# Second gate's seven products: another order, mixes formed inside PSUM banks, partial results subtracted inside the banks, weight rests cast in halves

## The chip, the core and the metric

One core of a Trainium2 chip runs the whole program. The time is the device time in microseconds of one execution; three runs of the kernel before gave 668.48, 669.56 and 670.56, median 669.56. TensorE is written PE, VectorE DVE, ScalarE ACT, GpSimd POOL, SyncE (which issues most DMAs) SP.

## What is computed

The reference is a two-layer encoder over 512 tokens of width 1024: a neighbourhood attention layer, then a latent attention layer. Each layer ends with a gate, and only the gate of the second layer is touched here:

```
h = x + y
gate = jax.nn.sigmoid(rmsnorm(h, ple_norm[i]) @ ple_w_gate[i])
x = h + gate * (p[i] @ ple_w_proj[i])
return rmsnorm(x, final_norm)          # after the second layer
```

## The kernel before

All matrix products are float32 products made of three float32r passes (high x high, low x high, high x low): an operand is a high copy (ACT) and a rest (the difference, by DVE or POOL). One 128 x 512 result is a PSUM bank; the pool tags are `mm` (2 banks), `S` (2), `T` (3), `O` (1).

**The second gate** (`gate_seven`, called for layer 1 from `run`) multiplies the 512 x 1024 state by the 1024 x 1024 weight as a 2 x 2 block product with seven products in place of eight. The state's four quarters are A (tokens 0-255, columns 0-511), B (same tokens, columns 512-1023), C and D (tokens 256-511). The seven left sides are 1: A, 2: B, 7: A-C, 6: A-C+D, 5: C-D, 3: B-(A-C+D), 4: D; the right sides are three quarters of the weight and four sums that DMAs formed in DRAM during the first layer. Each product runs for two row blocks `i` of 128 tokens; each needs 12 matmuls of 512 columns (or 24 of 256).

`keep_half(t, n, ps)` gets each quarter when PE has transposed it into a `T` bank: `out_proj` finishes row block t, column half n, DVE adds the residual (L428), scales it (`hg`, L1022), PE transposes it (L139). `operand(p, i, x)` makes the left side `X[p]`: ACT copies x (L538), DVE subtracts the copy (L539). Before the change the mixes live in one SBUF tile `mix`, named `F`; A-C and A-C+D are formed there (L556, L560), C-D too (L561), and D is copied to SBUF (L562). `mixed(p)` makes the left sides 6, 5, 4, 3 out of SBUF, so there DVE reads two SBUF tiles.

`gate_seven` takes the products in the order 1, 7, 6, 5, 4, 3, 2. `prep(p)` loads two weight pieces per product (SP, L588; three landing buffers `wraw`), ACT copies them (L589), POOL forms the rests (L590, 1024 columns at once): fourteen casts in all. Products 1 and 2 share a bank, so do 6, 5 and 3; what must be subtracted between them is held in SBUF: `s1`, `s17` (DVE, L650), `s6` (ACT L653, POOL L656). `finish` applies the sigmoid (ACT L595), multiplies with `pe` (DVE L598), adds to the residual `res` (DVE L600) and calls `done` at once: sum of squares (ACT L1066), small DVE and POOL steps (L1067, L1076), the scale by the final norm (DVE L1077, ACT L1078) and the output DMA.

Engines run their queues in order; each queue's order is fixed when the program is built, by a scheduler that follows the code, with `issue_after` holding PE's order of products.

Of the kernel before, what the change touches and what calls it, by code (L numbers as in the profile page):

```python
# [13 lines left out]
F32 = mybir.dt.float32  # L14
# [5 lines left out]
P = 128  # L20
# [20 lines left out]
class Trunk:  # L41
# [374 lines left out]
    def out_proj(self, wap, oT, res, after, last_mm):  # L416
        nc = self.nc
        for n in range(2):
            ws = [self.load_w(wap[n, c], 1024, extra=n == 1 or c == 3) for c in range(4)]
            for u, t in enumerate((0, 2, 1, 3) if n and self.wxn > 5 else range(NT)):  # L420
                ps = self.psum(("mm", "mm", "S", "S", "T", "O", "mm", "mm")[n * NT + u])
                L = lambda s, k: oT[s][k // 4][:, k % 4, t * P:(t + 1) * P]
                W = lambda s, k: ws[k // 2][s][:, (k % 2) * S:(k % 2 + 1) * S]
                m = self.by_chunk(L, W)
                with self.tc.issue_after(last_mm):
                    self.last_out = self.mms(ps, m)
                r = res[t][:, n * S:(n + 1) * S]
                nc.vector.tensor_tensor(out=r, in0=ps, in1=r, op=ALU.add)  # L428
                after(t, n)
# [111 lines left out]
    def keep_half(self, t, n, ps):  # L541

        nc = self.nc
        if (t, n) == (0, 0):
            self.X, self.B, self.Dd = {}, {}, {}
            self.F = self.bigtile("mix").bitcast(F32)
        i = t % 2
        ac, c = self.F[:, i, :], self.F[:, 2 + i, :]
        if t < 2:
            self.operand(1 + n, i, ps)  # L550
            if n:
                self.B[i] = self.temp("b")
            nc.scalar.activation(self.B[i] if n else ac, ps, AF.Copy)
        elif n == 0:
            nc.scalar.activation(c, ps, AF.Copy)
            nc.vector.tensor_tensor(out=ac, in0=ac, in1=ps, op=ALU.subtract)  # L556
            self.operand(7, i, ac)
        else:
            self.Dd[i] = self.temp("d")
            nc.vector.tensor_tensor(out=ac, in0=ac, in1=ps, op=ALU.add)  # L560
            nc.vector.tensor_tensor(out=c, in0=c, in1=ps, op=ALU.subtract)  # L561
            nc.scalar.activation(self.Dd[i], ps, AF.Copy)  # L562

    def mixed(self, p):

        for i in range(2):
            if p == 3:
                self.nc.vector.tensor_tensor(out=self.B[i], in0=self.B[i], in1=self.F[:, i, :], op=ALU.subtract)
            self.operand(p, i, {6: self.F[:, i, :], 5: self.F[:, 2 + i, :], 3: self.B[i], 4: self.Dd[i]}[p])

    def gate_seven(self, pool, layer, rh, res, after):
# [6 lines left out]
        def prep(p):  # L578
            nonlocal pieces
            W[p] = []  # L580
            src = self.quarter[layer][p] if p < 4 else self.sums[layer][p]
            for c in range(2):
                own = pieces % turns < 3
                pieces += 1
                raw = self.wp.tile([P, 1024], F32, name="wraw", tag="wraw", bufs=3)
                q, n = (self.wp, 3) if own else (pool, self.wxn)
                hi, lo = (q.tile([P, 1024], F32R, name=t, tag=t if own else "w4", bufs=n) for t in ("whi", "wlo"))
                nc.sync.dma_start(raw, src[c * P:(c + 1) * P])  # L588
                nc.scalar.activation(hi, raw, AF.Copy)  # L589
                nc.gpsimd.tensor_tensor(out=lo, in0=raw, in1=hi.bitcast(F32),  # L590
                                                                             op=ALU.subtract)
                W[p].append((hi, lo))

        def finish(t, n, x, o=0, wd=S):
            nc.scalar.activation(x, x, AF.Sigmoid, scale=rh[t])  # L595
            pe = pool.tile([P, S], F32, name="pe", tag="pe", bufs=4)[:, :wd]
            nc.sync.dma_start(pe, self.pe[layer][t][:, n * S + o:n * S + o + wd])
            nc.vector.tensor_tensor(out=x, in0=pe, in1=x, op=ALU.mult)  # L598
            r = res[t][:, n * S + o:n * S + o + wd]
            nc.vector.tensor_tensor(out=r, in0=r, in1=x, op=ALU.add)  # L600
            after(t, n, o, wd)

        def quarter(t, n, x, ps, other, op):
            nc.vector.tensor_tensor(out=x, in0=ps, in1=other, op=op)
            finish(t, n, x)

        mm = self.last_out
        order = (1, 7, 6, 5, 4, 3, 2)
        whole, parts = ((0, S),), ((0, 256), (256, 256))
        for p in order[:3]:  # L610
            prep(p)
        self.mixed(6)
        warm = self.small.tile([P, 1], F32, name="warm", tag="warm", bufs=1)
        nc.scalar.activation(warm, rh[3], AF.Sigmoid)
        for k, p in enumerate(order):
            if k == 0:
                prep(order[3])
            if k > 1 and k + 2 < len(order):
                prep(order[k + 2])
            if 0 < k < 4:  # L620
                self.mixed(order[k + 2])
            x = self.X[p]
            for i in range(2):
                cuts = parts if layer == 1 and i == 1 and p < 3 else whole
                if p == 1:
                    A[i] = [self.psum("O" if o else "mm") for o, wd in cuts]
                elif p in (7, 6, 4):
                    ps = self.psum({7: "T", 6: "S", 4: "T"}[p])
                    if p == 6:
                        Bk[i] = ps  # L630
                else:
                    ps = Bk[i]
                for h, (o, wd) in enumerate(cuts):
                    if p < 3:
                        ps = A[i][h]
                    m = [(x[:, 2 * s + i, k * P:(k + 1) * P], W[p][k // 2][r][:, k % 2 * S + o:k % 2 * S + o + wd])
                         for c in range(2) for s, r in ((0, 0), (1, 0), (0, 1)) for k in (2 * c, 2 * c + 1)]
                    for j, (l, r) in enumerate(m):
                        with self.tc.issue_after(mm.ins):
                            mm = nc.tensor.matmul(ps[:, :wd], l, r, start=j == 0 and p in (1, 7, 6, 4),  # L640
                                                  stop=j == 11 and p not in (1, 6, 5), skip_group_check=True)
                    if p == 1:
                        if o == 0:
                            s1[i] = self.temp("s1")
                        nc.scalar.activation(s1[i][:, o:o + wd], ps[:, :wd], AF.Copy)
                    elif p == 2:
                        finish(i, 0, ps[:, :wd], o, wd)
                    elif p == 7:
                        s17[i] = self.temp("s17")
                        nc.vector.tensor_tensor(out=s17[i], in0=ps, in1=s1[i], op=ALU.add)  # L650
                    elif p == 6:
                        s6[i] = self.temp("s6")
                        nc.scalar.activation(s6[i], ps, AF.Copy)  # L653
                    elif p == 5:
                        quarter(2 + i, 1, self.psum("T"), ps, s17[i], ALU.subtract)
                        nc.gpsimd.tensor_tensor(out=s6[i], in0=s17[i], in1=s6[i], op=ALU.subtract)  # L656
                    elif p == 4:
                        quarter(2 + i, 0, ps, ps, s6[i], ALU.add)
                    else:
                        quarter(i, 1, ps, ps, s1[i], ALU.subtract)  # L660
# [276 lines left out]
    def run(self):  # L937
# [64 lines left out]
        for layer in range(2):  # L1002
            with tc.tile_pool(name=f"out{layer}", bufs=4, reuse_waits="tile") as pool:
# [48 lines left out]
                else:  # L1052
                    mean = {}

                    def done(t, n, o, w):
# [22 lines left out]
                        nc.scalar.activation(r[:, f], r[:, f], AF.Copy, scale=rs)  # L1078
# [118 lines left out]
```

## Time and profile before

| | us |
|---|---|
| median of three runs | 669.56 |
| the profiled execution | 669.19 |
| its span, first to last instruction | 667.4 |
| first matmul of the second gate starts | 616.19 |
| last matmul ends | 658.58 |
| PE busy | 655.5 |
| POOL busy | 420.8 |
| ACT busy | 422.0 |
| DVE busy | 382.8 |

The span is the time between the first and the last instruction on the core; 1.8 us of the execution lie outside it. Times in the timelines count from the span's start. The granted TensorE clock is 0.997 over the span.

### The profile page before, as it was taken

To read this page: it belongs to the slowest core of one execution; us is meant where nothing else is said; L and a number is where in the kernel's file an instruction comes from. 1 tells how busy PE (TensorE), PEld (TensorE's weight loads), DVE (VectorE), ACT (ScalarE), POOL (GpSimd) and SP (SyncE) were. 2 spreads that over 40 slices of the span, in tenths; PEclk is the share of its full clock that TensorE was granted. 3 is DMA by queue.
4 is the path that set the end of the run, shared out by engine and by line. 5 is a ranking of instruction groups with operands and counts; after the bars stand their busy time and mean duration, and the time that the engine had idled before them with its cause. 6 is when DMAs were issued, how large, how long until landed. Compare 5 with 4: busy or idle time off the path is not lost.

```text
span 667.4 us, 10026 instructions
## 1 busy us (share of the span) xinstructions
PE 655.5 (98%) x3443; PEld 555.3 (83%) x3443; DVE 382.8 (57%) x817; ACT 422.0 (63%) x838; POOL 420.8 (63%) x340
## 2 busy tenths in 40 slices
PE   9999999999999999999999999999999999999994
PEld 6888888988988888888899888888888888888774
DVE  6290375737645514544525614888988875155977
ACT  7671686848767742543443635897989887446845
POOL 0395466876575765843154626786959786848893
PEclk9999999999999999999999999999999999999998
DMA  8949322966142146534243335120211222664423
GB/s 315 350 146 345 145 93 94 202 160 156 59 140 76 64 153 241 190 104 138 94 108 110 107 88 166 32 76 24 68 29 64 64 96 106 235 245 156 174 74 147
DMA packets 37682, 90.63 MB, mean 136 GB/s; under 512 B 4416, under 2 KB 13376, under 8 KB 37568
## 3 DMA queue, kind: packets, MB, share of 16 engines
q1 hardware_dynamic: 33040, 85.02, 37.1%
q0 software_dynamic: 4160, 4.19, 4.0%
q10 hardware_dynamic: 432, 0.79, 0.3%
q8 instruction: 27, 0.44, 0.3%
q14 instruction: 23, 0.19, 0.1%
HBM read 78.45 MB, written 16.78 MB: 143 GB/s over the span
## 4 chain that ended last, share of the span: by engine, by line
PE 91%; DVE 3%; ACT 2%; DMA 2%; issue 1%; POOL 1%; POOLq 0%; ACTq 0%
PE ps_mm L107 42%; PE ps_S L107 13%; PE ps_mm L727 7%; PE ps_T L139 6%; PE ps_O L838 4%; PE ps_T L107 3%; PE ps_O L107 3%; PE ps_T L238 2%; PE ps_O L402 2%; PE ps_mm L184 2%; PE ps_T L390 2%; PE ps_S L354 1%; PE ps_S L353 1%; PE ps_O L238 1%; DMA wraw<-gate 1%
## 5 line engine op out<-in xcount | busy, mean ns | idle before, releaser
L84 POOL TENSOR_TENSOR wwlo<-wraw,wwhi 128x1024 fp32r<-128x1024 f32 (+5 forms) x93 | 178.2, 1929 | 106.4 <-ACT wwhi L83 90.1
L83 ACT ACTIVATE wwhi<-wraw 128x1024 fp32r<-128x1024 f32 (+5 forms) x94 | 79.1, 863 | 73.6 <-issue 18.2
L823 POOL TENSOR_TENSOR ex<-ex,rc 128x512 f32<-128x512 f32 x64 | 66.3, 1046 | 25.2 <-DVE rc L822 18.1
L821 ACT ACTIVATE ex<-ps_S,mx 128x512 f32<-128x512 f32 x64 | 44.0, 687 | 12.2 <-DVE mx L819 11.1
L819 DVE TENSOR_REDUCE mx<-ps_S 128x1 f32<-128x512 f32 x64 | 43.7, 683 | 7.2 <-PE ps_S L107 6.8
L96 DVE TENSOR_TENSOR pt_lo<-ps_T,pt_hi 128x512 fp32r<-128x512 f32 x64 | 43.3, 682 | 7.7 <-ACT pt_hi L94 7.3
L376 POOL TENSOR_TENSOR ex<-ex,rc 128x128 f32<-128x128 f32 (+1 forms) x64 | 34.8, 583 | 18.1 <-DVE rc L372 18.1
L107 PE MATMUL ps_mm<-xh,wwhi 128*128 128x512 f32 x152 | 40.8, 399 | 0.0
L94 ACT ACTIVATE pt_hi<-ps_T 128x512 fp32r<-128x512 f32 x64 | 37.7, 594 | 4.4 <-PE ps_T L139 4.2
L139 PE MATMUL ps_T<-ident,ex 128*128 128x128 f32 x256 | 38.4, 272 | 0.0
L107 PE MATMUL ps_mm<-xl,wwhi 128*128 128x512 f32 x152 | 38.2, 390 | 0.0
L107 PE MATMUL ps_mm<-xh,wwlo 128*128 128x512 f32 x152 | 38.1, 391 | 0.0
L590 POOL TENSOR_TENSOR wlo<-wraw,whi 128x1024 fp32r<-128x1024 f32 x14 | 36.6, 2636 | 2.3 <-issue 2.3
L139 PEld LDWEIGHTS ps_T<-ident,ex 128*128 128x128 f32 x256 | 31.5, 140 | 7.7 <-POOL ex L823 0.4
L107 PE MATMUL ps_mm<-wwhi,hnT 128*128 128x512 f32 x128 | 35.5, 396 | 0.0
L205 DVE TENSOR_TENSOR u<-ps_O,u 64x512 f32<-64x512 f32 x32 | 21.9, 686 | 20.2 <-ACT u L204 19.7
L107 PEld LDWEIGHTS ps_mm<-xl,wwhi 128*128 128x128 f32 x152 | 28.4, 188 | 5.8
L107 PEld LDWEIGHTS ps_mm<-xh,wwlo 128*128 128x128 f32 x152 | 28.3, 188 | 5.8
L370 ACT ACTIVATE ex<-ex,mx 128x128 f32<-128x128 f32 (+1 forms) x64 | 30.3, 475 | 1.8 <-DVE mx L360 0.8
L107 PEld LDWEIGHTS ps_mm<-xh,wwhi 128*128 128x128 f32 x152 | 27.4, 188 | 4.7
L107 PE MATMUL ps_S<-ke,qe 96*128 96x512 f32 x96 | 29.2, 410 | 0.1
L107 PE MATMUL ps_S<-ko,qo 128*128 128x512 f32 x96 | 28.9, 409 | 0.0
(432 smaller groups left out, 1783.5 us busy)
## 6 DMA issues: line engine op xcount, KB each, us to landing
wraw<-na_qk SPq DMA_DIRECT2D x16, 512.0 KB, 3.3
pe<-pe SPq DMA_DIRECT2D x31, 256.0 KB, 2.8
wraw<-gate SPq DMA_DIRECT2D x14, 512.0 KB, 3.3
wraw<-na_v SPq DMA_DIRECT2D x8, 512.0 KB, 3.3
wraw<-na_o SPq DMA_DIRECT2D x8, 512.0 KB, 3.2
wraw<-mla_z SPq DMA_DIRECT2D x8, 512.0 KB, 3.5
wraw<-mla_o SPq DMA_DIRECT2D x8, 512.0 KB, 3.4
wraw<-sum SPq DMA_DIRECT2D x8, 512.0 KB, 3.2
```

Source lines behind the costliest of these rows:

```text
L83: nc.scalar.activation(hi[:, c], raw[:, c], AF.Copy)
L84: f = lambda e, c=c: e.tensor_tensor(out=lo[:, c], in0=raw[:, c], in1=hi[:, c].bitcast(F32), op=ALU.subtract)
L94: self.last_copy = nc.scalar.activation(hi, src, AF.Copy, scale=scale)
L96: nc.vector.tensor_tensor(out=lo, in0=src, in1=hi.bitcast(F32), op=ALU.subtract)
L107: last = self.last_mm = nc.tensor.matmul(out, l, r, start=i == 0, stop=i == n - 1)
L139: self.last_mm = self.nc.tensor.transpose(t[:, i * P:(i + 1) * P], b, self.ident)
L376: self.last_norm = nc.gpsimd.tensor_tensor(out=e, in0=e, in1=rc[:, qt:qt + 1].to_broadcast([P, e.shape[1]]), op=ALU.mult)
L590: nc.gpsimd.tensor_tensor(out=lo, in0=raw, in1=hi.bitcast(F32), op=ALU.subtract)
L727: self.last_mm = nc.tensor.matmul(PS[key], *terms[i], start=i == 0, stop=i == len(terms) - 1)
L819: nc.vector.reduce_max(mx, sp, axis=AX.X, negate=True)
L821: nc.scalar.activation(ex, sp, AF.Exp, bias=mx, accum_out=sm)
L823: nc.gpsimd.tensor_tensor(out=ex, in0=ex, in1=rc.to_broadcast([P, S]), op=ALU.mult)
```

## The change

Up to 596 us of the profiled execution the instructions of both programs stand in the same order on every engine. Behind that point:

- `out_proj` takes the row blocks 0, 1, 2, 3 in the second column half (before 0, 2, 1, 3).
- The mixes are formed in the `T` bank that PE transposed into: A-C overwrites the bank (L554), D's left side is made straight from its bank, then A-C+D overwrites it (L560) and gives left side 6 straight from the bank. C-D and B-(A-C+D) go to SBUF temporaries `c` and `b`.
- The products come in the order 1, 7, 2, 6, 5, 3, 4. Product 4 accumulates onto product 7's banks, product 3 onto 6+5. Between them DVE changes the banks in place (L616, L641), in place of `s6` on POOL.
- Halves of 256 columns are now used for products 7 and 4 at i = 1 (before: 1 and 2).
- Each weight rest is cast on POOL as two instructions of 512 columns (L589).
- `finish` calls `done` only behind the next sigmoid. The add to `res` goes to POOL (L603), but to DVE for products 3 and 4; the last scale of two row blocks goes from ACT to POOL (L1082).

```diff
-            for u, t in enumerate((0, 2, 1, 3) if n and self.wxn > 5 else range(NT)):
+            for u, t in enumerate(range(NT)):
...
         elif n == 0:
+            c = self.C[i] = self.temp("c")
             nc.scalar.activation(c, ps, AF.Copy)
-            nc.vector.tensor_tensor(out=ac, in0=ac, in1=ps, op=ALU.subtract)
-            self.operand(7, i, ac)
+            nc.vector.tensor_tensor(out=ps, in0=self.AC[i], in1=ps, op=ALU.subtract)
+            self.operand(7, i, ps)
+            nc.scalar.activation(self.AC[i], ps, AF.Copy)
         else:
-            self.Dd[i] = self.temp("d")
-            nc.vector.tensor_tensor(out=ac, in0=ac, in1=ps, op=ALU.add)
-            nc.vector.tensor_tensor(out=c, in0=c, in1=ps, op=ALU.subtract)
-            nc.scalar.activation(self.Dd[i], ps, AF.Copy)
+            self.operand(4, i, ps)
+            nc.vector.tensor_tensor(out=self.C[i], in0=self.C[i], in1=ps, op=ALU.subtract)
+            nc.vector.tensor_tensor(out=ps, in0=self.AC[i], in1=ps, op=ALU.add)
+            self.operand(6, i, ps)
+            nc.vector.tensor_tensor(out=self.B[i], in0=self.B[i], in1=ps, op=ALU.subtract)
...
-                nc.gpsimd.tensor_tensor(out=lo, in0=raw, in1=hi.bitcast(F32),
-                                                                             op=ALU.subtract)
+                for o in (slice(0, S), slice(S, 2 * S)):
+                    nc.gpsimd.tensor_tensor(out=lo[:, o], in0=raw[:, o], in1=hi[:, o].bitcast(F32), op=ALU.subtract)
...
-        def finish(t, n, x, o=0, wd=S):
-            nc.scalar.activation(x, x, AF.Sigmoid, scale=rh[t])
+        def finish(t, n, x, o=0, wd=S, last=False):
+            sg = nc.scalar.activation(x, x, AF.Sigmoid, scale=rh[t])
+            while behind:
+                with self.tc.issue_after(sg.ins):
+                    behind.pop()()
...
-            nc.vector.tensor_tensor(out=x, in0=pe, in1=x, op=ALU.mult)
+            nc.vector.tensor_tensor(out=x if last else pe, in0=pe, in1=x, op=ALU.mult)
             r = res[t][:, n * S + o:n * S + o + wd]
-            nc.vector.tensor_tensor(out=r, in0=r, in1=x, op=ALU.add)
-            after(t, n, o, wd)
+            (nc.vector if last else nc.gpsimd).tensor_tensor(out=r, in0=r, in1=x if last else pe, op=ALU.add)
+            behind.append(lambda: after(t, n, o, wd))
...
-        order = (1, 7, 6, 5, 4, 3, 2)
+        order = (1, 7, 2, 6, 5, 3, 4)
...
+                    elif p == 7:
+                        nc.vector.tensor_tensor(out=ps, in0=ps, in1=s1[i][:, c], op=ALU.add)
                         if o == 0:
+                            s17[i] = self.temp("s17")
+                        nc.scalar.activation(s17[i][:, c], ps, AF.Copy)
                     elif p == 6:
                         s6[i] = self.temp("s6")
                         nc.scalar.activation(s6[i], ps, AF.Copy)
+                        for (a, b, o), t in C.items():
+                            if (a, b) == (7, i):
+                                sub(t, t, s6[i][:, o:o + t.shape[1]])
                     elif p == 5:
-                        quarter(2 + i, 1, self.psum("T"), ps, s17[i], ALU.subtract)
-                        nc.gpsimd.tensor_tensor(out=s6[i], in0=s17[i], in1=s6[i], op=ALU.subtract)
-                    elif p == 4:
-                        quarter(2 + i, 0, ps, ps, s6[i], ALU.add)
+                        q = self.psum("mm" if i else "T")
+                        sub(q, ps, s17[i])
+                        sub(ps, ps, s1[i])
+                        finish(2 + i, 1, q)
```

How the queues read, at three places.

DVE before, from the second column half of row block 3 on to the left side of product 6, i = 1 (`X_6512` is the left side of product 6, `X_6575` of 5, `X_6622` of 4, `X_6670` of 3):

```order
L560 TENSOR_TENSOR mix<-mix,ps_T 128x512
L561 TENSOR_TENSOR mix<-mix,ps_T 128x512
L568 TENSOR_TENSOR b<-b,mix 128x512
L539 TENSOR_TENSOR X_6622<-d,X_6622 128x512
L539 TENSOR_TENSOR X_6670<-b,X_6670 128x512
L539 TENSOR_TENSOR X_6512<-mix,X_6512 128x512
L650 TENSOR_TENSOR s_6593<-ps_T,s_6544 128x512
```

The same place now, for row block 3 (`X_6433` is the left side of product 6, `X_6428` of 4, `X_6711` of 3, `X_6591` of 5):

```order
L539 TENSOR_TENSOR X_6428<-ps_T,X_6428 128x512
L559 TENSOR_TENSOR c<-c,ps_T 128x512
L560 TENSOR_TENSOR ps_T<-a,ps_T 128x512
L539 TENSOR_TENSOR X_6711<-b,X_6711 128x512
L641 TENSOR_TENSOR ps_T<-ps_T,s_6560 128x512
L539 TENSOR_TENSOR X_6591<-c,X_6591 128x512
L641 TENSOR_TENSOR ps_T<-ps_T,s_6575 128x256
L539 TENSOR_TENSOR X_6433<-ps_T,X_6433 128x512
```

Left side 6 is read from the `T` bank, and only left sides 3 and 5 are still made from SBUF.

ACT before, around the copies `s_6640` and `s_6655` of product 6's banks (L653), with the last weight copies (`whi`):

```order
L589 ACTIVATE whi<-wraw 128x1024 x2
L653 ACTIVATE s_6640<-ps_S 128x512
L589 ACTIVATE whi<-wraw 128x1024
L653 ACTIVATE s_6655<-ps_S 128x512
L589 ACTIVATE whi<-wraw 128x1024
L595 ACTIVATE ps_T<-ps_T,rs 128x512
```

And now (the copies are `s_6729` and `s_6745`, L647):

```order
L587 ACTIVATE whi<-wraw 128x1024
L595 ACTIVATE ps_mm<-ps_mm,rs 128x512
L587 ACTIVATE whi<-wraw 128x1024
L1069 ACTIVATE sq,ss<-r 128x512
L647 ACTIVATE s_6729<-ps_S 128x512
L647 ACTIVATE s_6745<-ps_S 128x512
```

Both copies now stand behind the last weight copy and behind the first sum of squares.

POOL now, from the casts of products 5 and 3 (eight halves) on to the last cast:

```order
L589 TENSOR_TENSOR wlo<-wraw,whi 128x512 x8
L603 TENSOR_TENSOR r<-r,pe 128x512
L589 TENSOR_TENSOR wlo<-wraw,whi 128x512 x2
L603 TENSOR_TENSOR r<-r,pe 128x512
L589 TENSOR_TENSOR wlo<-wraw,whi 128x512 x2
L1073 TENSOR_TENSOR r<-r,gn 128x512 x2
```

Before, this stretch held four casts of 1024 columns (L590), then L656, a cast, L656, a cast. The first add to `res`, which that sum of squares reads, now stands behind the twelfth cast.

More of the change, by code (lines that the diff above doesn't have):

```diff
@@ L589, in prep @@
                 nc.scalar.activation(hi, raw, AF.Copy)
[L590 to L591 removed]
+                for o in (slice(0, S), slice(S, 2 * S)):
+                    nc.gpsimd.tensor_tensor(out=lo[:, o], in0=raw[:, o], in1=hi[:, o].bitcast(F32), op=ALU.subtract)
                 W[p].append((hi, lo))
[L594 to L595 removed]
+        behind = []
@@ L623, in gate_seven @@
             for i in range(2):
[L624 to L635, printed above, removed]
+                for o, wd in halves if i and p in (7, 4) else ((0, S),):
+                    c = slice(o, o + wd)
+                    if p in banks:
+                        C[p, i, o] = self.psum("O" if o else banks[p])[:, :wd]
+                    ps = C[home.get(p, p), i, o]
```

61 lines of the change are left out of this document (30 added, 31 removed).

## The prediction

> **What bounds the kernel now.** I read the page first: busy shares, the slices, the chain that ended last.
>
> ```profile
> PE 655.5 (98%) x3443; PEld 555.3 (83%) x3443; DVE 382.8 (57%) x817; ACT 422.0 (63%) x838; POOL 420.8 (63%) x340
> PE   9999999999999999999999999999999999999994
> PE 91%; DVE 3%; ACT 2%; DMA 2%; issue 1%; POOL 1%; POOLq 0%; ACTq 0%
> ```
>
> PE is busy in every slice but the last, and carries 91% of the chain. So only two things can pay: gaps of PE, and the stretch behind its last matmul. The order before and now is the same up to 596 us, so I read on in PE's timeline of the second gate, where the change lies.
>
> ```profile
> 616.19 1.17 PE L640 MATMUL ps_mm<-whi,X 128*128 128x512 f32 x4
> 621.89 0.60 PE L139 MATMUL ps_T<-ident,hg 128*128 128x128 f32 x4
> 622.25 1.18 PE L640 MATMUL ps_T<-whi,X 128*128 128x512 f32 x4
> 627.90 1.09 PE L640 MATMUL ps_S<-whi,X 128*128 128x512 f32 x4
> ...
> 630.24 0.63 PE L640 MATMUL ps_S<-wlo,X 128*128 128x512 f32 x2
> 630.70 0.63 PE L640 MATMUL ps_S<-whi,X 128*128 128x512 f32 x2
> 632.72 0.72 PE L640 MATMUL ps_S<-whi,X 128*128 128x512 f32 x2 [1.39 <-DVE X L539]
> ...
> 643.05 0.61 PE L640 MATMUL ps_T<-wlo,X 128*128 128x512 f32 x2
> 644.43 1.17 PE L640 MATMUL ps_T<-whi,X 128*128 128x512 f32 x4 [0.77 <-DVE r L600]
> ...
> 658.19 0.39 PE L640 MATMUL ps_O<-wlo,X 128*128 128x256 f32 x2
> ```
>
> Two matmuls take 0.46 us of PE's time (630.24 to 630.70). So after 630.70 the next was due at 631.16 and came at 632.72: **1.56 us late**, waiting for the left side of product 6. After 643.05 the next was due at 643.51 and came at 644.43: **0.92 us late**, waiting for a `T` bank. PE ends at 658.19 + 0.39 = 658.58; without both gaps it would be 656.10. The 8.8 us from there to the span's end (667.4) are the tail.
>
> Why was left side 6 late? DVE's and POOL's timelines:
>
> ```profile
> 621.64 2.88 DVE L539 TENSOR_TENSOR X<-mix,X 128x512 fp32r<-128x512 f32 x1
> 624.63 0.67 DVE L568 TENSOR_TENSOR b<-b,mix 128x512 f32<-128x512 f32 x1
> 628.56 2.90 DVE L539 TENSOR_TENSOR X<-d,X 128x512 fp32r<-128x512 f32 x1
> 631.99 0.68 DVE L539 TENSOR_TENSOR X<-mix,X 128x512 fp32r<-128x512 f32 x1
> ```
> ```profile
> 598.72 10.39 POOL L590 TENSOR_TENSOR wlo<-wraw,whi 128x1024 fp32r<-128x1024 f32 x4
> 613.07 2.38 POOL L590 TENSOR_TENSOR wlo<-wraw,whi 128x1024 fp32r<-128x1024 f32 x1
> 615.93 8.05 POOL L590 TENSOR_TENSOR wlo<-wraw,whi 128x1024 fp32r<-128x1024 f32 x3
> 625.69 5.22 POOL L590 TENSOR_TENSOR wlo<-wraw,whi 128x1024 fp32r<-128x1024 f32 x2
> ```
>
> The same subtraction takes 0.68 us while POOL is idle (631.99; POOL's casts end at 630.91) and 2.88 to 2.90 while POOL casts. 628.56 + 2.90 = 631.46 lies 0.55 behind the end of POOL's cast: DVE stood until that cast was over. Subtractions that read PSUM show no such wait, though casts ran beside most of them:
>
> ```profile
> L539 DVE TENSOR_TENSOR X<-mix,X 128x512 fp32r<-128x512 f32 x6 | 9.6, 1596 | 2.0 <-ACT X L538 2.0
> L539 DVE TENSOR_TENSOR X<-ps_T,X 128x512 fp32r<-128x512 f32 x4 | 2.7, 686 | 0.0
> ```
>
> **The change, part by part.** The sum is made against the profiled execution: span 667.4, device time 669.19, of which 1.8 lie outside the span; the median of the runs, 669.56, is 0.37 above it.
>
> *Matmuls and cuts.* 168 matmuls' worth of 512 columns stays, 24 of them still as pairs of halves, at other places: 0.
>
> *Mixes in the bank, other order: gap 1 goes, -1.56.* Product 6 comes fourth in place of third, so PE reaches it 5.6 us later. Left side 6 at i = 1 is the fifteenth DVE instruction behind the last `hg`. That `hg` is needed by the transposes at 621.89; 15 times 0.686 puts the left side at 632.2; three of the fifteen read SBUF alone, and if each waited for a whole half cast (1.3, below) it would be 636.1. PE needs it at 627.90 + 5.6 + 2.8 = 636.3. Cover 0.2 us at worst, 4.1 at best; behind it each late us costs one. ACT's extra copies (four of 0.6) lie in its idle time.
>
> On slower PSUM reads the trace has 0.686 us against 0.67 from SBUF (row 624.63): 0.02 each. [...]
>
> *Product 4 onto product 7's banks: gap 2 goes, -0.92.* It needs no new `T` bank any more. DVE must have subtracted `s6` by then, three instructions behind the copies and 11 us (two products) ahead of PE. Product 3 now needs its bank after two subtractions (2 x 0.69) while PE is busy 2.8 us with the other row block: 0, with 1.4 us to spare.
>
> *The new wait, at product 5: +1.5.* Product 5 overwrites product 6's sum, so PE waits for the ACT copy `s6`. Before, ACT made it at once. Now it stands behind the last weight copy and a sum of squares, which reads the first POOL add, which is queued behind twelve casts. I price both roads.
>
> ```profile
> L84 POOL TENSOR_TENSOR wwlo<-wraw,wwhi 128x512 fp32r<-128x512 f32 x13 | 16.6, 1300 | 1.2 <-ACT wwhi L83 1.2
> L84 POOL TENSOR_TENSOR ww<-wraw,ww 128x1024 fp32r<-128x1024 f32 x5 | 11.9, 2394 | 9.0 <-ACT ww L83 9.0
> L1070 POOL TENSOR_TENSOR r<-r,gn 128x512 f32<-128x512 f32 x4 | 5.1, 1287 | 1.8 <-ACT sq L1066 1.8
> ```
> ```profile
> wraw<-gate SPq DMA_DIRECT2D x14, 512.0 KB, 3.3
> 641.23 1.06 ACT L589 ACTIVATE whi<-wraw 128x1024 fp32r<-128x1024 f32 x1 [5.28 <-DMA wraw<-gate]
> 644.32 0.63 ACT L1066 ACTIVATE sq<-r 128x512 f32<-128x512 f32 x1 [1.49 <-DVE r L600]
> 633.88 0.61 ACT L653 ACTIVATE s<-ps_S 128x512 f32<-128x512 f32 x1
> ```
>
> POOL's road: the first ten casts took 10.39 + 2.38 + 8.05 + 5.22 = 26.04 us, 23.9 by the bare 2.394, so 2.1 of lock waits. Twenty halves take 26.0 bare. Of eleven DVE instructions that read SBUF alone in that stretch about seven stay, so I keep 1.3 of the 2.1: the tenth cast ends 1.3 later, at 630.91 + 1.3 = 632.2. POOL's 2.3 us of idle time there go, since ACT reaches those weights sooner. Casts eleven and twelve add 5.2 + 0.3: 637.7; the add 1.29: 639.0. Transfer's road: the last landing buffer comes free with the eleventh cast (634.9), 3.3 to landing, 1.06 for the copy: 639.2. Then the square (0.63 and about 0.1 for its accumulator) and `s6` (0.61): 640.6. PE ends product 6 at 627.90 + 11.2 = 639.1 and waits about 1.5. Bounds: 0, if POOL is 1.5 faster (halves at half of 2.394 are 0.1 less each, 2.4 over 24); above, 3.3, if that transfer lands late as it did before:
>
> ```profile
> 636.16 5.04 DMA wraw<-gate
> q8 instruction: 1, 0.02, 2.2%
> ```
>
> That row of the chain is the last weight transfer: 5.04 us against a median of 3.3. The DMA view of that stretch (636.1 to 641.3) shows one fetch of instructions among its packets; the stretch 628 to 631.4, where a transfer took 3.2, has none. If a fetch hits the last transfer again, the wait is 1.5 + 1.8 = 3.3. I take 1.5, the median's value.
>
> *Tail: 0.* Before:
>
> ```profile
> 658.86 0.43 ACT L595 ACTIVATE ps_O<-ps_O,rs 128x256 f32<-128x256 f32 x1
> 659.97 0.42 DVE L598 TENSOR_TENSOR ps_O<-pe,ps_O 128x256 f32<-128x256 f32 x1
> 660.64 0.41 DVE L600 TENSOR_TENSOR r<-r,ps_O 128x256 f32<-128x256 f32 x1
> 661.30 0.48 DVE L1062 CUSTOM_DVE_ANT_0 sq<-r,mn 128x256 f32<-128x256 f32 x1
> 661.87 0.99 POOL L1076 TENSOR_TENSOR rs<-mn,half 128x1 f32<-128x1 f32 x1 [0.52 <-DVE mn L1062]
> 662.90 0.75 DVE L1077 SCALAR_TENSOR_TENSOR r<-r,rs,gn 128x512 f32<-128x512 f32 x1 [0.44 <-POOL rs L1076]
> ```
>
> That ends 663.65, 5.07 behind PE, then 3.75 for the output. Now the same chain ends it. DVE no longer drags a backlog, but in the last 3 us it has two more scales of 0.75 among those rows, and POOL's new scales can lock them. The bare chain is 0.43 + 0.42 + 0.41 + 0.56 + 0.55 to 0.99 + 0.75, about 3.4: bounds -1.6; a locked scale +1.0. I take 0, nearest to the row.
>
> Sum: -1.56 - 0.92 + 1.5 + 0 = **-1.0 us**: 668.2 in that execution, 668.6 on the median's scale.
>
> **Rivals.** Differences of 0.3% (2.0 us) are about what a measurement of this kernel can tell from no change.
>
> *A, the last transfer lands late again.* For it: PE fetches its instructions at about the same place of its queue, and the transfer now starts 1.3 us earlier (634.9), PE is 1.6 earlier. Against: the median is 3.3. Sum -1.0 + 1.8 = +0.8: 670.4.
>
> *B, POOL keeps up.* Halves shorten each lock that DVE waits for, POOL is 1.5 ahead of my sum, product 5 waits for nothing: -2.5, 667.1.
>
> *C, slower: POOL becomes the engine that PE waits for at product 5.* Where a POOL instruction of 512 columns was locked out by DVE it took longer:
>
> ```profile
> L656 POOL TENSOR_TENSOR s<-s,s 128x512 f32<-128x512 f32 x2 | 3.0, 1508 | 0.0
> ```
>
> At 1.42 per half, 24 halves end 2.9 later than mine, the wait is 4.4, with a late transfer up to 5.2: +1.9 to +2.7, say 671.8. It decides from a wait of 4.5 us. Against: before, 2.1 us of locks came with eleven DVE rows, 0.2 each; 2.9 more would take some fifteen rows more, and there are fewer. [...]
>
> *D, the change doesn't do what it says.* If DVE's in-bank instructions waited for POOL too, ten of them would cost up to 1.3 each, 6 us beyond the cover, and gap 1 would return. The row of 686 ns speaks against it. Gap 1 back with gap 2 gone and the new wait: +0.6, 670.2.
>
> **How the numbers follow.** Forecast (wait of about 1 to 2 us) 0.46, A 0.27, B 0.12, C 0.11, D 0.04. B holds the gains of over 2.0 (below 667.6), with a little of the tail's lower bound: faster 0.13. C gives slower 0.11. The rest, 0.76, lies within 0.3%. The range reaches from B (667.0) to +1.5 (671.1), between A and C.
>
> **What would show it.** Gap 1: no wait of PE for an `X` in products 6, 5, 3, 4; the left sides from `T` banks near 0.69 us. Gap 2: no wait for a bank at product 4. New wait: PE's first matmul of product 5 released by ACT's `s6`, ACT idle for POOL's add or for the last `wraw`; the POOL casts by halves near 1.3. The tail: 5 us from PE's end to the last DVE scale. I am wrong if PE waits elsewhere, above all for POOL's rests, or if the wait at product 5 is missing or over 4 us.

## Result: 0.8 us less, both gaps of PE gone, one new wait

The changed kernel takes 668.03 us (median of 14 runs, 667.14 to 669.03) against 668.85 (668.22 to 670.58) for the kernel before: ratio 0.9983, 95% interval [0.9975, 0.9991]. That is 0.8 us less, inside the 0.3% that the forecast calls the same. 668.6 was forecast, counted from the three runs known then (669.56); as a ratio 0.9986. The profiled execution of the changed kernel took 668.41 us with a span of 666.3 (before: 669.19 and 667.4). So of the 1.1 us by which the span is shorter only 0.8 reach the device time: in the 14 runs of the changed kernel 2.1 to 2.2 us lie outside the span, in those of the kernel before 1.7 to 1.9. One difference is on record there: a fetch of 8 KB of instructions on queue 14, which came at 660.5 us before and now comes at 667.9, 1.6 us behind the last instruction (DMA view of the changed kernel from 667 to 669 us):

```profile
q14 instruction: 1, 0.01, 1.0%
```

That this fetch costs the 0.3 us was not tested.

The page of the changed kernel, busy times and chain:

```profile
PE 655.2 (98%) x3443; PEld 555.2 (83%) x3443; DVE 372.0 (56%) x815; ACT 421.8 (63%) x838; POOL 424.5 (64%) x358
PE 93%; POOL 2%; DMA 1%; issue 1%; DVE 1%; ACT 1%; POOLq 0%; DVEq 0%
```

DVE does 10.8 us less and POOL 3.7 more; PE still carries the chain. PE's timeline in the second gate (start, duration, line, operation, count, in brackets the idle time ahead and its releaser):

```profile
616.55 1.08 PE L635 MATMUL ps_mm<-whi,X 128*128 128x512 f32 x4
633.68 1.09 PE L635 MATMUL ps_S<-whi,X 128*128 128x512 f32 x4
636.48 1.09 PE L635 MATMUL ps_S<-whi,X 128*128 128x512 f32 x4
...
638.82 0.62 PE L635 MATMUL ps_S<-wlo,X 128*128 128x512 f32 x2
640.34 1.20 PE L635 MATMUL ps_S<-whi,X 128*128 128x512 f32 x4 [0.90 <-ACT s L647]
...
656.83 0.39 PE L635 MATMUL ps_O<-wlo,X 128*128 128x256 f32 x2
```

Product 6 begins at 633.68, its second row block at 636.48. There is one wait, at the first matmul of product 5: due at 638.82 + 0.46 = 639.28, it came at 640.34, **1.06 us late**, and ACT's copy `s6` released it. PE ends at 656.83 + 0.39 = 657.22; before it was 658.58. The difference of 1.36 is 1.56 + 0.92 for the two gaps, less 1.06 for the new wait, less 0.06.

DVE's groups of the subtraction that makes left sides, from 595 us on (count, sum, mean ns), and two rows of its timeline:

```profile
L539 DVE TENSOR_TENSOR X<-ps_T,X 128x512 fp32r<-128x512 f32 x10 | 6.8, 687 | 4.0 <-ACT X L538 4.0
L539 DVE TENSOR_TENSOR X<-b,X 128x512 fp32r<-128x512 f32 x2 | 3.3, 1643 | 0.8 <-ACT X L538 0.8
L539 DVE TENSOR_TENSOR X<-c,X 128x512 fp32r<-128x512 f32 x2 | 3.0, 1495 | 0.0
617.95 1.43 DVE L1025 SCALAR_TENSOR_TENSOR hg<-r,rowb,gp 128x512 f32<-128x512 f32 x1
630.29 0.68 DVE L539 TENSOR_TENSOR X<-ps_T,X 128x512 fp32r<-128x512 f32 x1
```

Read from the bank it takes 0.687 us, whatever POOL does: six of the ten lie inside POOL's casts, each 0.68 to 0.69. From SBUF (`b`, `c`) it takes 1.5 to 1.6 on average. A lock is, as in the forecast, what such an instruction takes beside a POOL row beyond its 0.68 with POOL idle; the rows show how long it is, not what holds it. The last two rows are the last `hg` and left side 6 of the second row block; that one is ready at 630.97, needed at 636.48, **5.5 us to spare**.

The chain between 631 and 641 us names what product 5 waited for (start, duration, what):

```profile
632.21 1.50 POOL wlo L589 x2
633.72 4.38 DMA wraw<-sum
638.13 1.06 ACT whi L587
639.19 0.30 ACT sq L1069
639.80 0.49 ACT s L647
```

POOL frees the landing buffer, the last weight transfer is issued at 633.72 and takes 4.38 us, ACT copies it, squares, and only then copies `s6`. POOL's own rows:

```profile
599.00 10.05 POOL L589 TENSOR_TENSOR wlo<-wraw,whi 128x512 fp32r<-128x512 f32 x8
612.75 2.54 POOL L589 TENSOR_TENSOR wlo<-wraw,whi 128x512 fp32r<-128x512 f32 x2 [1.73 <-ACT whi L587]
616.29 8.01 POOL L589 TENSOR_TENSOR wlo<-wraw,whi 128x512 fp32r<-128x512 f32 x6
625.23 11.43 POOL L589 TENSOR_TENSOR wlo<-wraw,whi 128x512 fp32r<-128x512 f32 x8
636.62 1.29 POOL L603 TENSOR_TENSOR r<-r,pe 128x512 f32<-128x512 f32 x1
618.78 1.75 POOL L589 TENSOR_TENSOR wlo<-wraw,whi 128x512 fp32r<-128x512 f32 x1
```

The last row is one of the third row's six halves by itself: it ran beside the last `hg` and took 1.75 us in place of 1.29. The add that the square reads ends at 637.91, before the last weight copy begins (638.13): POOL's road was not the later one. The tail, from DVE's timeline:

```profile
653.86 1.63 DVE L1080 SCALAR_TENSOR_TENSOR r<-r,rs,gn 128x512 f32<-128x512 f32 x1
657.07 1.44 DVE L1080 SCALAR_TENSOR_TENSOR r<-r,rs,gn 128x512 f32<-128x512 f32 x1
658.89 0.41 DVE L601 TENSOR_TENSOR ps_O<-pe,ps_O 128x256 f32<-128x256 f32 x1
661.75 0.75 DVE L1080 SCALAR_TENSOR_TENSOR r<-r,rs,gn 128x512 f32<-128x512 f32 x1 [0.66 <-POOL rs L1079]
```

It ends at 662.50, 5.28 us behind PE (before: 5.07). Two of the scales take 1.63 and 1.44 in place of 0.75, beside POOL's new scales (653.90 and 656.92, 1.04 each).

### The profile page after: what moved, and what is told of

Same layout as the page of the kernel before. It is cut to its first block, busy times and chain, and to the rows that moved or that the text cites. A ratio compares the mean times of both kernels' runs of the same rounds, so it can differ in the third digit from the quotient of the medians.

```text
span 666.3 us, 10037 instructions
## 1 busy us (share of the span) xinstructions
PE 655.2 (98%) x3443; PEld 555.2 (83%) x3443; DVE 372.0 (56%) x815; ACT 421.8 (63%) x838; POOL 424.5 (64%) x358
## 4 chain that ended last, share of the span: by engine, by line
PE 93%; POOL 2%; DMA 1%; issue 1%; DVE 1%; ACT 1%; POOLq 0%; DVEq 0%
PE ps_mm L107 42%; PE ps_S L107 13%; PE ps_mm L730 6%; PE ps_T L139 6%; PE ps_O L841 4%; PE ps_T L107 3%; PE ps_O L107 3%; PE ps_T L238 2%; PE ps_O L402 2%; PE ps_S L635 2%; PE ps_mm L184 2%; PE ps_T L390 2%; PE ps_mm L635 1%; PE ps_S L354 1%; PE ps_S L353 1%
## 5 line engine op out<-in xcount | busy, mean ns | idle before, releaser
L589 POOL TENSOR_TENSOR wlo<-wraw,whi 128x512 fp32r<-128x512 f32 x28 | 37.1, 1355 | 1.7 <-ACT whi L587 1.7
```

The source lines that it names most:

```text
L589: nc.gpsimd.tensor_tensor(out=lo[:, o], in0=raw[:, o], in1=hi[:, o].bitcast(F32), op=ALU.subtract)
```

## The experiments

The theory was: both gaps are gone for good; PE's wait at product 5 is the last weight transfer, seen through ACT's queue; that transfer is long because a fetch of PE's instructions lies beside it; and POOL's new scales cost the tail something. The rivals: POOL is what product 5 waits for; the transfer is long for another reason; only the halves, or only the bank mixes, closed gap 1.

A measure that leaves out what happens ahead of the change is the **gate**: from PE's first matmul of the second gate to its last. The table has every trace; "late" is PE's lateness at product 5, "transfer" the last weight transfer, the tail runs from PE's end to DVE's last scale. The ratio is to the kernel before, measured beside each. The kernel before begins its gate with other rows in front, so its 42.39 compares only roughly.

| kernel | gate, us | late | transfer | tail | median, us | ratio [95%] |
|---|---|---|---|---|---|---|
| before | 42.39 | (gaps 1.56 + 0.92) | 5.04 | 5.07 | 668.85 | |
| changed | 40.67 | 1.06 | 4.38 | 5.28 | 668.03 | 0.9983 [0.9975, 0.9991] |
| changed again (e10) | 40.11 | 0.48 | 3.7 | 5.29 | 667.86 | 0.9986 [0.9977, 0.9995] |
| e1 s6 first | 39.59 | 0 | 4.2 | 5.28 | 667.61 | 0.9980 [0.9971, 0.9988] |
| e2 fetch moved | 39.52 | 0 | 3.2 | 5.28 | 667.40 | 0.9977 [0.9968, 0.9987] |
| e3 whole rests | 39.51 | 0 | 3.3 | 5.28 | 667.59 | 0.9975 [0.9965, 0.9986] |
| e4 scale on ACT | 40.32 | 0.68 | 4.0 | 4.73 | 667.39 | 0.9975 [0.9965, 0.9985] |
| e5 mixes in SBUF | 41.03 | 1.41 | 3.4 | 5.28 | 668.77 | 0.9994 [0.9985, 1.0003] |
| e12 order alone | 41.43 | 1.78 | 3.5 | 5.28 | 669.12 | 1.0001 [0.9992, 1.0010] |
| e7 before + halves | 41.12 | (product 5: 1.00) | 3.2 | 4.63 | 668.09 | 0.9981 [0.9972, 0.9990] |
| e8 = e1 + e4 | 39.61 | 0 | 3.8 | 4.73 | 666.84 | 0.9965 [0.9952, 0.9977] |
| e9 = e3 + e4 | 39.51 | 0 | 3.2 | 4.74 | 666.78 | 0.9965 [0.9953, 0.9978] |
| e11 = e1 + e3 + e4 | 39.51 | 0 | 3.3 | 4.74 | 666.85 | 0.9972 [0.9961, 0.9983] |

**e1: ACT copies s6 ahead of the last weight.**

```diff
-                prep(order[k + 3])
+                prep(order[k + 3], (0,) if k == 3 else (0, 1))
...
-                        nc.scalar.activation(s6[i], ps, AF.Copy)
+                        held = nc.scalar.activation(s6[i], ps, AF.Copy)
...
+                        if i:
+                            prep(4, (1,), held.ins)
```

(The second argument of `prep` now picks the half of the weight; with the third, ACT's copy of it is issued behind that instruction.)

> The changed kernel, with ACT's last weight copy put behind the two copies of s6. Theory: PE's 1.06 us at product 5 is the last weight transfer, waited for through ACT's queue only. With the copy behind s6, PE's first matmul of product 5 is at most 0.3 us late, PE ends about 1.0 us earlier (656.2 in the trace), and the time is about 667.0 us, 1.0 below the changed kernel's 668.0. The last weight's copy then starts near 640.4 and its rests end near 644, far ahead of product 4 (651). Rival: PE waits for POOL's add (through the square of row block 0), so it is still 0.7 us or more late, and the time stays at 668.0. Second rival: PE gains 1.0 us and the tail gives it back (last DVE scale still near 662.5).

ACT's timeline of this kernel:

```profile
638.74 0.63 ACT L1075 ACTIVATE sq<-r 128x512 f32<-128x512 f32 x1 [1.81 <-POOL r L607]
639.37 0.58 ACT L651 ACTIVATE s<-ps_S 128x512 f32<-128x512 f32 x1
640.32 0.60 ACT L651 ACTIVATE s<-ps_S 128x512 f32<-128x512 f32 x1 [0.37 <-PE ps_S L639]
640.81 1.06 ACT L591 ACTIVATE whi<-wraw 128x1024 fp32r<-128x1024 f32 x1
```

The last weight copy stands behind both copies of `s6`, and PE does not wait at all, although the transfer took 4.2 us again. The gate is 1.08 us shorter. So the wait was the weight, through ACT's queue. The first rival falls by a narrow margin: the square now waits for POOL's add, and the first `s6` is ready at 639.95, when PE's first matmul of product 5 was due (640.06). The median fell by 0.42 against the first measurement of the changed kernel and by 0.25 against the second (e10), not by the expected 1.0. Two things tell against the 1.0: executions differ far ahead of the gate (this trace lost 0.84 us at 77 us, last section), and the changed kernel does not always wait 1.06 (e10).

**e2: the instruction fetch moved.**

```diff
-            for i in range(NWARM):
-                nc.tensor.matmul(ps, *ones, start=True, stop=True)
+            for i in range(NWARM + 16):
+                nc.tensor.matmul(ps[:, :208], ones[0], ones[1][:, :208], start=True, stop=True)
```

> The changed kernel with 27 warm-up matmuls of 208 columns at the start in place of 11 of 512 (the same columns, 16 matmuls more), so that PE's later instruction fetches come some 3.7 us earlier against the work. Nothing else moves. Theory: the fetch at 633.7 to 634.6 slowed the last weight transfer (4.38 us). It now falls near 630, beside another transfer, the last one lands in 3.1 to 3.4 us, PE is 0 to 0.3 us late at product 5, and the time is about 667.1 us, 0.9 below the changed kernel's 668.0. Rival: the transfer is slow because of the other data transfers (the weight transfer just ahead, the pe rows), so it still takes 4.2 us or more, PE is 1 us late, and the time stays at 668.0.

The DMA view of the changed kernel from 633.6 to 638.2 us: bytes moved in 40 equal slices, the queues (packets, MB, share of 16 engines), and the issue with its time to landing:

```profile
GB/s 427 285 72 0 0 142 0 0 0 214 142 214 36 36 36 321 321 392 392 321 427 427 392 356 214 72 36 0 36 36 0 36 36 36 0 36 0 0 0 0
q8 instruction: 1, 0.02, 1.2%
wraw<-sum SPq DMA_DIRECT2D x1, 512.0 KB, 4.4
```

The same view of e2, from 633.6 to 638, where there is no q8 row:

```profile
GB/s 372 335 298 37 0 0 0 0 0 0 186 223 149 74 37 335 223 410 372 410 410 298 484 372 372 298 112 0 0 0 0 0 0 0 0 0 0 0 0 0
q1 hardware_dynamic: 188, 0.64, 41.2%
wraw<-sum SPq DMA_DIRECT2D x1, 512.0 KB, 3.2
```

In the changed kernel nearly all of the weight is there after 26 slices; then single packets follow, 36 GB/s in a slice of 0.115 us (4.1 KB), for 1.1 us. That one of the sixteen engines was behind is the author's reading; the view does not tell them apart. In e2 the fetch (q8) comes at 631.0 to 631.9 and the transfer, issued at 633.76, ends in one piece. The fetch's packet takes 1.2% of 16 x 4.6 us of the engines' time, 0.9 us. The last weight transfer of all the traces of this study says the same. With the fetch 0.4 to 1.1 us behind the issue it took 3.7 (e10), 3.8 (e8), 4.0 (e4), 4.2 (e1), 4.4 (changed) and 5.0 (before); with the fetch just ahead of the issue 3.4 (e5), with it 2.5 to 2.9 us behind 3.5 (e12), 3.3 (e3, e11) and 3.2 (e9), and with none beside it 3.2 (e2, e7). How far it is delayed inside the first group is not explained by the place of the fetch alone: some transfers at 607 to 611 us with a fetch 0.2 to 0.6 us behind their issue took 3.5 to 3.7 (before, e2, e7). PE was not late, and the gate is 1.15 us shorter: this rival falls too (667.40 us, where 667.1 was expected). Sixteen matmuls more brought the fetch some 3.3 us forward (from 634.3 to 631.0), and PE waited for it in neither trace: its one wait in the changed kernel's gate is at 640.34, and e2's gate of 39.52 us has none. But with the fetch 0.4 to 1.1 us behind its issue the last weight transfer took 0.5 to 1.8 us more (3.7 to 5.0 in place of 3.2).

**e3: whole rests.**

```diff
-                for o in (slice(0, S), slice(S, 2 * S)):
-                    nc.gpsimd.tensor_tensor(out=lo[:, o], in0=raw[:, o], in1=hi[:, o].bitcast(F32), op=ALU.subtract)
+                nc.gpsimd.tensor_tensor(out=lo, in0=raw, in1=hi.bitcast(F32), op=ALU.subtract)
```

> The changed kernel with each weight rest as one POOL instruction of 1024 columns again. Theory: the order alone closes gap 1, since left side 6 had 5.5 us to spare; locks of up to 2.9 us in place of 1.8 take at most 4 of these. POOL is about 0.19 us faster per weight (2.39 against 2 x 1.29), so the last landing buffer comes free 1 to 2 us earlier, the last transfer lands by 637, and PE's lateness at product 5 shrinks from 1.06 us to 0 to 0.4: time 667.0 to 667.4. Rival: the halves are what closed gap 1. Then PE waits again for a left side in product 2 or 6, 0.5 to 1.5 us, and the time is 668.5 or more.

Two DVE groups and one POOL row of this kernel:

```profile
L539 DVE TENSOR_TENSOR X<-b,X 128x512 fp32r<-128x512 f32 x2 | 4.5, 2242 | 0.4 <-ACT X L538 0.4
L539 DVE TENSOR_TENSOR X<-c,X 128x512 fp32r<-128x512 f32 x2 | 3.8, 1914 | 0.0
624.88 10.41 POOL L588 TENSOR_TENSOR wlo<-wraw,whi 128x1024 fp32r<-128x1024 f32 x4
```

DVE's left side 3 (`b`), locked, grows from 1.64 to 2.24 on average and nobody is late for it. POOL does four weights in 10.41 us in place of 11.43, the last transfer is issued 0.75 us earlier (632.97) and has only 0.4 us to go when the fetch comes at 635.85: no wait. Gap 1 stays closed. With the bank mixes in place, the halves buy nothing that the runs show and cost POOL a quarter of a microsecond per weight, locks included. The time of 667.59 lies a little above the 667.0 to 667.4 expected; this trace too lost time at 77 us.

**e4: the final scale back on ACT.**

```diff
-                        if seven and n:
-                            nc.gpsimd.tensor_tensor(out=r[:, f], in0=r[:, f], in1=rs.to_broadcast([P, S]), op=ALU.mult)
-                        else:
-                            nc.scalar.activation(r[:, f], r[:, f], AF.Copy, scale=rs)
+                        nc.scalar.activation(r[:, f], r[:, f], AF.Copy, scale=rs)
```

> The changed kernel with the final scale by rs of the last two row blocks back on ACT. Theory: POOL's scales locked DVE's (1.63 and 1.44 us in place of 0.75); they return to 0.75, and the tail from PE's last matmul to DVE's last scale shrinks from 5.28 to about 5.0: time 667.7 to 668.0, no more, since the bare chain behind PE's last matmul sets the end. Rival: the scale of 0.7 us on ACT comes between the last sigmoid and what it waits for, and the tail grows by 0.3 to 0.6 us: 668.3 to 668.6.

DVE's rows that answer to those of the tail above:

```profile
656.46 0.75 DVE L1080 SCALAR_TENSOR_TENSOR r<-r,rs,gn 128x512 f32<-128x512 f32 x1
657.98 0.43 DVE L601 TENSOR_TENSOR ps_O<-pe,ps_O 128x256 f32<-128x256 f32 x1
660.80 0.75 DVE L1080 SCALAR_TENSOR_TENSOR r<-r,rs,gn 128x512 f32<-128x512 f32 x1 [0.66 <-POOL rs L1079]
```

Here PE ends at 656.82, and the multiplication of the last piece starts 1.16 us behind it; in the changed kernel it was 1.67 (658.89 - 657.22), behind the scale of 1.44. The tail is 4.73, 0.55 shorter, twice what was expected, and 667.39 lies below the range expected. (The rest of this kernel's gain in the trace, 0.35, is the transfer of 4.0.)

**e5 and e12: the mixes back in SBUF, with halves and without.** e5:

```diff
-            nc.vector.tensor_tensor(out=ps, in0=self.AC[i], in1=ps, op=ALU.subtract)
-            self.operand(7, i, ps)
-            nc.scalar.activation(self.AC[i], ps, AF.Copy)
+            nc.vector.tensor_tensor(out=self.AC[i], in0=self.AC[i], in1=ps, op=ALU.subtract)
+            self.operand(7, i, self.AC[i])
...
-            nc.vector.tensor_tensor(out=ps, in0=self.AC[i], in1=ps, op=ALU.add)
-            self.operand(6, i, ps)
-            nc.vector.tensor_tensor(out=self.B[i], in0=self.B[i], in1=ps, op=ALU.subtract)
+            nc.vector.tensor_tensor(out=self.AC[i], in0=self.AC[i], in1=ps, op=ALU.add)
+            self.operand(6, i, self.AC[i])
+            nc.vector.tensor_tensor(out=self.B[i], in0=self.B[i], in1=self.AC[i], op=ALU.subtract)
```

e12 has this and e3's edit together.

> The changed kernel with the mixes made in SBUF again (the copies a changed in place, the left sides 7 and 6 and the mix b read from there), everything else as changed. Theory: the new order alone gives product 6 the time; eight DVE instructions that read PSUM now read SBUF alone and stand for POOL up to 1.8 us in place of 0.69, so left side 6 at i = 1 is ready 2 to 5 us later than at 630.97, still ahead of 636.5. PE is not late in product 6 by more than 0.3 us. The locks also cost POOL, so the last transfer and s6 come later, PE is 1.0 to 2.0 us late at product 5: time 668.0 to 669.0. Rival: the mixes in the bank are what closed gap 1. Then PE is late by 0.5 us or more for a left side in product 7, 2 or 6, and the time is above 669.

> The changed kernel with the mixes in SBUF and with whole weight rests, so that of the cures of gap 1 only the new order (and the banks it uses) is left. Theory: DVE's left sides of SBUF now take up to 2.9 us each, as in the kernel before; left side 6 at i = 1 is ready at 633 to 636, still ahead of the 636.5 at which PE needs it, so gap 1 stays closed. POOL's rests are slowed by DVE as before, the last transfer is issued near 634 to 635.5, and PE is 0 to 1.5 us late at product 5: 667.5 to 668.6. Rival: the order alone isn't enough; PE waits 0.5 us or more for a left side in product 2 or 6, and the time is 668.6 or more.

PE's only wait in e5, and its left sides 7 and 6:

```profile
641.09 1.19 PE L634 MATMUL ps_S<-whi,X 128*128 128x512 f32 x4 [1.25 <-ACT s L646]
L539 DVE TENSOR_TENSOR X<-a,X 128x512 fp32r<-128x512 f32 x4 | 6.3, 1576 | 2.4 <-ACT X L538 2.4
```

The same of e12, with left sides 4 (`ps_T`) and 6 (`a`) of the second row block and the rows of POOL and ACT ahead of product 5:

```profile
641.09 1.21 PE L633 MATMUL ps_S<-whi,X 128*128 128x512 f32 x4 [1.62 <-ACT s L645]
628.20 0.68 DVE L539 TENSOR_TENSOR X<-ps_T,X 128x512 fp32r<-128x512 f32 x1
632.12 2.90 DVE L539 TENSOR_TENSOR X<-a,X 128x512 fp32r<-128x512 f32 x1
638.51 1.29 POOL L601 TENSOR_TENSOR r<-r,pe 128x512 f32<-128x512 f32 x1 [1.23 <-DVE pe L599]
639.83 0.63 ACT L1067 ACTIVATE sq<-r 128x512 f32<-128x512 f32 x1 [0.78 <-POOL r L601]
```

In neither does PE wait for a left side: even with 2.90 us for left side 6 it is ready at 635.02, ahead of 636.5. **Gap 1 stays closed without the bank mixes and without the halves.** That it is the order alone isn't shown, though: ahead of left side 6, e12 still makes a left side 4 straight from its bank in 0.68 us, where the kernel before made one from SBUF (`X<-d`) in 2.90. With 1.5 us to spare one more such lock (2.90 - 0.68 = 2.22) could have opened the gap again.

But the locks return at product 5. In e5 it is POOL that is slowed; one of its rows:

```profile
625.93 11.99 POOL L588 TENSOR_TENSOR wlo<-wraw,whi 128x512 fp32r<-128x512 f32 x8
```

Its first 24 halves take 34.9 us (11.44 + 2.55 + 8.92 + 11.99) in place of 32.0, and the last transfer is issued 1.7 us later: PE is 1.41 us late. In e12 DVE's left side 3 lasts until 637.83 (635.28 + 2.55), its product for POOL's add comes late, and the square waits 0.78 us for POOL behind a weight copy that was late by itself: PE is 1.78 us late, and the last part of that is the road over POOL's add. That eats the two gaps: 669.12 us, the time of the kernel before and above the 667.5 to 668.6 expected. By the ratios the bank mixes are worth 0.7 us with halves (e5 against the changed kernel; the intervals overlap) and 1.7 us without (e12 against e3), and they earn it at product 5 and not at product 6.

**e7: the kernel before, with halves and nothing else.**

```diff
-                nc.gpsimd.tensor_tensor(out=lo, in0=raw, in1=hi.bitcast(F32),
-                                                                             op=ALU.subtract)
+                for o in (slice(0, S), slice(S, 2 * S)):
+                    nc.gpsimd.tensor_tensor(out=lo[:, o], in0=raw[:, o], in1=hi[:, o].bitcast(F32), op=ALU.subtract)
```

> The kernel before with the weight rests in halves and nothing else of the change. Theory: a lock lasts at most as long as POOL's instruction at hand, so DVE's left sides that read SBUF fall from up to 2.9 to at most 1.8 us; gap 1 (1.56 us) shrinks to 0 to 0.6. Gap 2 (0.92, a T bank) stays or grows with the later start of the weights: 667.6 to 668.4. Rival: POOL's longer total (0.19 us more per weight) and DVE's backlog leave gap 1 as it is (over 1 us): 668.8 or more.

PE at the first matmuls of product 5 and of product 4 (block 1):

```profile
634.39 0.62 PE L640 MATMUL ps_S<-wlo,X 128*128 128x512 f32 x2
635.85 1.20 PE L640 MATMUL ps_S<-whi,X 128*128 128x512 f32 x4 [0.83 <-ACT s L653]
...
644.19 0.62 PE L640 MATMUL ps_T<-wlo,X 128*128 128x512 f32 x2
644.64 1.07 PE L640 MATMUL ps_T<-whi,X 128*128 128x512 f32 x4
```

Gap 1 is gone without a new order, gap 2 with it (644.19 + 0.46 = 644.65), and a wait of 1.00 us for `s6` stands in their place (due at 634.85), with 0.24 more at the second row block: the same exchange. 668.09 us, 0.9981: this one edit gains on the old order as much as the whole change does, within the intervals. The theory of the locks held: DVE's longest left side between 618 and 634 us takes 1.78, where it was 2.90 before. That gap 2 would go was not expected.

**e8, e9, e11: repairs together; e10: the changed kernel again.** e8 has the edits of e1 and e4, e9 those of e3 and e4, e11 all three.

> The changed kernel with two repairs: ACT's last weight copy behind the copies of s6, and the final scales by rs on ACT. Theory: both add up. No wait of PE at product 5 (1.06 us of the changed kernel's trace), tail 4.7 us in place of 5.28: 1.6 us below the changed kernel, 666.4, and 2.4 below the kernel before. Rival: one hides the other (the later weight copy delays ACT's sigmoids or POOL's adds, so the tail is 5.2 or more): 667.0 or above.

> The changed kernel with whole weight rests and the final scales by rs on ACT. Theory: the last transfer is issued about 0.7 us earlier and lands ahead of the instruction fetch, PE is not late at product 5, the tail is 4.7 us: the same 666.4 as with s6 first. Rival: without halves DVE's longer locks (2.2 us each for left side 3) push the stretch around product 5, or the fetch hits the last transfer: PE late by 0.5 us or more, 667.0 or above.

> The changed kernel itself once more, beside the next one on the same chip, for a direct comparison. Theory: its gate from PE's first matmul to its last takes 40.3 to 40.7 us again, with the instruction fetch beside the last weight transfer (3.8 to 4.4 us to landing) and PE 0.5 to 1.1 us late at product 5; the tail is 5.28. What differs between executions lies ahead of the gate (stalls at 77 and 413 us). About 0.9985 of the kernel before. Rival: the wait at product 5 was an accident of one execution; then this trace shows none and a gate of 39.6 us.

> The changed kernel with all three repairs: ACT's last weight copy behind s6, whole weight rests, final scales on ACT. Theory: the first two take away the same wait, so together they bring no more than either: gate 39.5 us, tail 4.7, about 0.9965 of the kernel before, the same as the pairs. Rival: they add up, a further 0.5 us or more: 0.9955 or below.

The changed kernel again, at product 5 (due at 638.72 + 0.46 = 639.18):

```profile
639.66 1.20 PE L635 MATMUL ps_S<-whi,X 128*128 128x512 f32 x4 [0.32 <-ACT s L647]
```

The wait is there again, but 0.48 us, with a transfer of 3.7: both at or a little below the ends that were named. With 0.48 for the wait and 0.55 for the tail the repairs should bring 1.03, and they do: e11 takes 666.85 us (666.65 to 666.95) beside 667.86 (667.49 to 668.89) for the changed kernel on the same chip, e8 and e9 666.84 and 666.78. The expected 666.4 had the wait at 1.06. The three are alike, as two cures of one wait must be; the rival of e11 falls. They beat both kernels: e8 by a ratio of 0.9965 [0.9952, 0.9977] to the kernel before.

## Why the forecast held, step by step

- **Gap 1 (-1.56): right.** Shown by the left side ready 5.5 us early. The bounds of 632.2 to 636.1 for it were too late: it came at 630.97. Locks were met (left sides 3 and 5 took 1.80, 1.76 and 1.19 us ahead of it), but the count began too late: the last `hg` was done at 619.38 (617.95 + 1.43), 2.5 us ahead of the 621.89 of the transposes, and unlocked DVE instructions of 512 columns follow each other every 0.60 us (619.30, 619.90, 620.49) where the sum took 0.686. e12, with longer locks, came to 635.02, inside the bounds. The rows of the three kernels: a left side from SBUF takes up to 2.90 us beside rests of 2.39 (before and e12), up to 1.80 beside halves of 1.29 (2.22 and 1.12 beyond its 0.68), and one from the bank 0.687. What the two engines wait for in each other was not shown.
- **Slower PSUM reads (0.02 each): right that it is little.** In e12 left side 5 (SBUF, unlocked) took 677 ns and those from the bank 685: 0.008 us.
- **Gap 2 (-0.92): right**, no wait at product 4. e7 shows that less waiting of DVE would have closed it as well.
- **The new wait (+1.5): right in kind, and two errors in it nearly cancelled.** It is ACT's `s6` behind the last weight, as written. But POOL ran 1.0 to 1.2 us ahead of the sum: the tenth weight was cast at 631.19 and not 632.2, the transfer issued at 633.72 and not 634.9, and POOL's add ended at 637.91 and not 639.0. The locks were not what was missing: three of the first twenty halves took 1.75 us in place of 1.29, 1.4 us in all, as kept. But undisturbed halves follow each other every 1.26 us (10.05 for eight) where the sum took 1.30, and POOL's small rows between the casts took 0.6 us less (2.6 in place of 3.2). And the transfer took 4.38 and not 3.3, which is rival A's event. That the two came together is luck, and the +1.5 owes its nearness to it. 1.06 came out, in the second trace 0.48. e2 shows A's cause, e1 that the wait can be taken away at no cost.
- **The tail (0): too low by 0.21 in the trace**, within its bounds of -1.6 and +1.0. e4 takes the sum apart: POOL's scales cost 0.55, and without them the tail is 0.34 shorter than before (4.73 against 5.07). That need not be the new tail's doing: e7, with the old tail, has 4.63.
- **The sum (-1.0)**: span -1.1, of the executions profiled -0.78, of the medians -0.82. The sum took what lies outside the span as fixed at 1.8; it grew by 0.3.
- **Rivals.** A's event happened and its price did not, because POOL ran ahead of the sum. That lead is most of what B asked for (1.5); the late transfer ate it, and in e2, where the transfer is short, PE waits for nothing at product 5. C did not occur, but e5 shows its mechanism as soon as the mixes leave the banks: 1.45 us per half, where C had 1.42, and a wait of 1.41 where C needed 4.5. D is refuted by the 0.687.

Where did the gain of two closed gaps go? 2.48 us went, 0.5 to 1.06 came back at product 5, 0.2 in the tail, 0.3 outside the span. What was not tried: the bank mixes or the new order by themselves in the kernel before; a change of `s6` itself, so that product 5 overwrites nothing.

## What to carry to other kernels

Here a DVE subtraction of 128x512 that read one operand from PSUM took 0.687 us whatever POOL did, and one that read SBUF alone up to 1.8 us beside POOL instructions of 512 columns and 2.9 beside those of 1024. Moving an operand to a bank and making POOL's instructions shorter are two cures of one illness, and they don't add up: by the ratios, against the new order with neither (e12), halves bring 0.5 us (e5; the intervals overlap), banks 1.7 (e3), both 1.2 (the changed kernel, whose last transfer met the fetch). When a wait goes, look for the next late thing in the same buffers: here a copy that frees a bank stood in ACT's queue behind a copy that waits for a transfer, and putting the copy that somebody waits for first (e1) cost nothing. Undo a change part by part even when it brings what was foretold: one of its parts (the scale on POOL) cost 0.55 us in the trace, and another (the halves) showed no worth beside the rest.

## What the runs showed of the hardware that was not expected

- A fetch on q8 is one packet of 16 KB (27 of them with 0.44 MB in the kernel before); the one beside the last weight transfer took 0.9 us (changed) to 1.9 (before). Where it came 0.4 to 1.1 us behind the issue of the last weight transfer (512 KB), that transfer took 3.7 to 5.0 us; with the fetch moved away it took 3.2 (e2). With 16 matmuls more at the kernel's start it came 3.3 us earlier (e2), so an edit far ahead can move it.
- Executions differ ahead of the change. PE has a stall at 77 us in some traces and not in others, and one at 413 us; e1's and e9's:

```profile
77.90 1.39 PE L107 MATMUL ps_mm<-xh,wwhi 128*128 128x512 f32 x5 [0.84 <-DVE sb L270]
```
```profile
413.65 0.50 PE L107 MATMUL ps_S<-ke,qe 96*128 96x512 f32 x1 [0.59 <-DMA qe<-rl]
```

The changed kernel's trace has neither. In e7, which has both, PE begins the gate 1.36 us later than in the kernel before, more than the whole effect here: a gain of this size has to be read from the gate in the trace, or from many runs.
